# Modulation dots in the middle of each product group, their rows in the gated outputs' ring, activation sums from float32 tiles

## The chip, the core and the metric

One NeuronCore of a Trainium2 chip runs the kernel. The metric is device time in microseconds from launch to end, as the median of several runs; lower is better. Weights and inputs are float32 and lie in HBM. PE is the matmul engine, DVE the vector engine, ACT the activation engine, POOL the GpSimd engine, SP the queue that issues most loads.

## What is computed

One transformer block over 512 tokens of width 1024, batch 1. Six modulation vectors come from a small product with the conditioning vector c:

```python
mod = jnp.einsum('bd,de->be', silu(c), w_ada) + b_ada
shift1, scale1, gate1, shift2, scale2, gate2 = jnp.split(mod, 6, axis=-1)
hmix = rmsnorm(x, g_norm1) * (1 + scale1) + shift1
sb_q, sb_k, sb_v, r_q, r_k, r_v, r_g, br = jnp.split(hmix @ w_in, IN_SPLITS, axis=-1)
o_sb = stick_breaking_attention(sb_q, sb_k, sb_v)           # 16 heads of 64
o_ret = silu(r_g) * head_rmsnorm(retention(rotary(r_q), rotary(r_k) / 16, r_v))   # 4 heads, qk 256, v 512
g_sb, g_ret = jnp.split(sigmoid(br + b_branch), 2, axis=-1)
x = x + gate1 * ((g_sb * (o_sb @ w_proj_sb) + g_ret * (o_ret @ w_proj_ret)) @ w_out)
hffn = rmsnorm(x, g_norm2) * (1 + scale2) + shift2
a, u = jnp.split(hffn @ w_ffn_in, 2, axis=-1)
out = rmsnorm(x + gate2 * ((silu(a) * u) @ w_ffn_out), g_final)
```

## The kernel before

Every matmul operand is held as a high and a low part (`hi`, `lo`, both in the reduced float32 type fp32r). A product is three matmuls: hi by hi, hi by lo, lo by hi. `weight()` loads 512 KB into the ring "raw", ACT rounds it to "whi" (L206), DVE subtracts for "wlo" (L208). `high()` and `low()` (L849, L853) do the same for pieces that are sums.

A ring is a tag of a tile pool with a fixed number of buffers: "araw" has 2, "raw" 3, "whi" and "wlo" 4 each, "s" 8, "o" 8, "t" 7, "q" 8. A tile takes a buffer when one is free, and whatever fills it waits for the last reader of the tile that had it. Outside blocks under `manual_schedule` a planner orders each engine's instructions ahead of time, by program order as the priority, by free buffers, and by its own estimates of durations; at run time each engine follows that order. `tc.issue_after(ins)` puts an edge from `ins` to those instructions in its block that run on the engine of `ins`: the dots, being DVE work, come behind `ins` on DVE, but the loads of their rows do not.

The stages that matter here, in order:

- The opening (L440 to L557, order by hand): squares of x, the row scale r1, the modulation dots 0 to 7, and per 128 rows of the width the modulated activations: `h_t` (L424) writes x times gain times r1 into a "t" tile, `h_hi` and `h_lo` add the shift and split the result into `hs[n]`. For n = 0 the shift is added into the float32 tile itself.
- `sv_acts` (L860): the four sums of activation quarters S1 to S4 that the seven-product groups need. Each is built on DVE from high and low parts of `hs`, 256 columns at a time (`each`, L868 to L872), and is split by `parts` (L874).
- Four groups. Each covers `ret_gate` of one retention head (gate product L760, transposes L764, the gated outputs `ys` in four "s" tiles), `ret_proj` (its projection, summed into `spill` in DRAM), and `seven` (L973): a product of 1024 by 1024 made of seven half-size products, A11, A12, S2, S3, A22, S1, S4 in this order, with weight sums `w1` to `w7`. `b11` and `b22` are raw quarters in "s", `b12` in "araw", `b21` in "raw". Head h + 1's `ret_scores` and `ret_out` run within `seven`. The last group makes the values of the stick-breaking attention.
- The attention stage: `sb_qk` projects two heads, `heads` works through 16 heads, `mix` computes the branch gates, whose tiles are in "araw".
- The loop over `w_proj_sb` (L1120), then w_out, the second norm, the feed-forward part.

A modulation dot (`ada`, L246): a 512 KB row block of w_ada lands in a tile, DVE multiplies it by the broadcast `cact` and sums along the row (L256), reads the sum, adds the bias (L259). A pair is two such dots. Pairs 0 to 7 are in the opening; `later` holds pairs 8 to 23, which `ada_after(ins)` takes one at a time. Before the change these go: two in each `ret_gate` of heads 1 to 3, four in each `ret_proj` of heads 1 and 2, and the last two in the loop over `w_proj_sb`. All of them load into "araw".

Of the kernel before, what the change touches and what calls it, by code (L numbers as in the profile page):

```python
# [11 lines left out]
F32 = mybir.dt.float32  # L12
# [3 lines left out]
ALU = mybir.AluOpType  # L16
# [3 lines left out]
P = 128  # L20
D = 1024
S = 512
KT = D // P
# [92 lines left out]
def kernel(  # L116
# [9 lines left out]
    nc = tc.nc  # L126
# [9 lines left out]
    def nm(s):  # L136
        uid[0] += 1
        return f"{s}_{uid[0]}"
# [13 lines left out]
    def tmp():  # L152
        return apool.tile([P, S], F32, tag="t", bufs=BUFS["t"], name=nm("t"))
# [4 lines left out]
    def small(n, dt=F32):  # L158
        return cpool.tile([P, n], dt, tag=f"sm{n}{dt}", bufs=BUFS["sm"], name=nm("sm"))

    def f(ap):
        return ap.bitcast(F32)
# [15 lines left out]
    for j in range(KT):  # L178
# [9 lines left out]
    nc.vector.memset(ones, 1.0)  # L188
    eps = cpool.tile([P, 1], F32, name="eps")
    nc.vector.memset(eps, EPS)  # L190
    nc.gpsimd.affine_select(ident, ones, pattern=[[1, P]], compare_op=ALU.is_equal, fill=0.0, base=0,
                            channel_multiplier=-1)
    mod = cpool.tile([P, 48], F32, name="mod")
# [5 lines left out]
    def load_raw(src, n, tag="raw"):  # L199
        raw = wpool.tile([P, WCOLS], F32, tag=tag, bufs=BUFS[tag], name=nm(tag))  # L200
        nc.sync.dma_start(raw[:, :n], src[:, :n])
        return raw
# [32 lines left out]
    def gemm(o, w, acts, start=True, stop=True, t0=0, t1=S, ks=None):  # L235

        hi, lo = w
        n = len(acts)
        for k in ks or range(n):
            a = acts[k]  # L240
            ah, al = a if isinstance(a, tuple) else (a[:, 0, :], a[:, 1, :])
            mm3(o, hi[:, k, :], lo[:, k, :], ah[:, t0:t1], al[:, t0:t1],
                start and k == 0, stop and k == n - 1)


    def ada(n):  # L246

        pair_cols = []
        for half, c in enumerate(ADA[n]):
            if n < KT:  # L250
                raw = apool.tile([P, D], F32, tag="s", bufs=BUFS["s"], name=nm("sraw"))
                nc.sync.dma_start(raw, wada[2 * n + half])
            else:
                raw = load_raw(wada[2 * n + half], D, "araw")
            col = small(1)
            nc.vector.scalar_tensor_tensor(  # L256
                raw, raw, 1.0, cact, op0=ALU.mult, op1=ALU.mult, accum_out=col
            )
            nc.vector.tensor_add(mod[:, c : c + 1], col, sm[:, SM_BADA + c : SM_BADA + c + 1])  # L259
            pair_cols.append(mod[:, c : c + 1])  # L260
        return pair_cols
# [138 lines left out]
        cols_[n, 0] = o[:, 0:1]  # L400

    def mod_shift(n):
        sh = small(1)
        b = SM_BADA + n
        nc.scalar.activation(sh, cols_[n, 0], AF.Identity, bias=sm[:, b : b + 1])  # L405
        mods[n, 0] = sh
# [15 lines left out]
    ALL = slice(0, S)  # L422

    def h_t(n, hv=ALL):  # L424
        if n not in ts:
            ts[n] = tmp()
        nc.vector.scalar_tensor_tensor(ts[n][:, hv], xts[n][:, hv], mods[n, 1], r1[:, hv],
                                       op0=ALU.mult, op1=ALU.mult)

# [151 lines left out]
    def sb_qk(p):  # L581
        qp, kp = ps(), ps()
        gemm(qp, weight(("sq", p)), hs)
        gemm(kp, weight(("sk", p)), hs)
        sb_qk_store(p, qp, kp)

    def causal(t, c):

# [169 lines left out]
    def ret_gate(h, banks, y, sgs, between=lambda: None):  # L758
        for b, (o, sg) in enumerate(zip(banks, sgs)):
            nc.vector.scalar_tensor_tensor(sg, o, y[:, b : b + 1], sg, op0=ALU.mult, op1=ALU.mult)  # L760
        ys = []
        for e, o in enumerate((psz(), psz(), psz(), psa())):
            for b, sg in enumerate(sgs):
                nc.tensor.transpose(o[:, b * P : (b + 1) * P], sg[:, e * P : (e + 1) * P], ident)  # L764
            hl = pair("s")
            ins = split(hl[:, 0, :], hl[:, 1, :], o)
            ys.append(hl)
            between()
            if e % 2 and h:
                ada_after(ins)  # L770
        return ys

    spill = dpool.tile([8, P, S], F32, name="spill")
# [3 lines left out]
    def ret_proj(h, ys, before=lambda i: None):  # L777

        for i in range(4):
            before(i)  # L780
            hi, lo = weight(("pr", h, i))
            low = last_low[0]
            for c in range(2):
                o = ps()
                gemm(o, (hi[:, :, c * P : (c + 1) * P], lo[:, :, c * P : (c + 1) * P]), ys)
                t = otile()
                nc.scalar.activation(t, o, AF.Copy)
                if h == 0:
                    nc.sync.dma_start(spill[2 * i + c], t)
                else:  # L790
                    nc.gpsimd.dma_start(spill[2 * i + c], t, accum_op=ALU.add)
            if h in (1, 2):
                ada_after(low)


    def gate(i):

# [17 lines left out]
    gains2 = []  # L815
    later = list(range(8, 24))

    def ada_after(ins):
        with tc.issue_after(ins.ins):
            n = later.pop(0)  # L820
            sh, sc = ada(n)
            if 12 <= n < 20:
                j = n - 12
                gains2.append((gain(sc, sm[:, SM_G2 + j : SM_G2 + j + 1]), sh))
# [7 lines left out]
    def raw_quarter(tag):  # L832
        return apool.tile([P, 2 * S], F32, tag=tag, bufs=BUFS[tag], name=nm(tag))
# [16 lines left out]
        return hi  # L850

    def low(t, hi, lo):
        nc.vector.tensor_sub(lo, t, f(hi))  # L853
        return hi, lo


# [3 lines left out]
    def sv_acts():  # L860
        def part_of(lo, kh, th):
            return [hs[4 * kh + k][:, lo, th * 256 : th * 256 + 256] for k in range(4)]

        acts = {}
        for key, kh, th in (("A11", 0, 0), ("A12", 1, 0), ("A22", 1, 1)):
            acts[key] = part_of(0, kh, th), part_of(1, kh, th)

        def each(dst, op, src, kh, th, lo, swap=False):  # L868
            for k, a in enumerate(part_of(lo, kh, th)):
                d = slice(k * 256, k * 256 + 256)  # L870
                x, y = src[:, d] if src is not None else f(part_of(0, kh, th)[k]), f(a)
                nc.vector.tensor_tensor(dst[:, d], *((y, x) if swap else (x, y)), op=op)  # L872

        def parts(t, tag):  # L874
            n = 2 if tag == "o" else 4
            his, los = [], []
            for k in range(0, 4, n):
                hi, lo = (
                    apool.tile([P, n * 256], F32R, tag=tag, bufs=BUFS[tag], name=nm(tag)) for _ in range(2)
                )  # L880
                src = t[:, k * 256 : (k + n) * 256]
                nc.scalar.activation(hi, src, AF.Copy)
                nc.vector.tensor_sub(lo, src, f(hi))
                his += [hi[:, i * 256 : i * 256 + 256] for i in range(n)]
                los += [lo[:, i * 256 : i * 256 + 256] for i in range(n)]
            return his, los

        yield acts
        a21, t = raw_quarter("s"), raw_quarter("s")
        each(a21, ALU.add, None, 0, 1, 1)  # L890
        yield
        each(t, ALU.add, a21, 1, 1, 0)
        yield
        each(t, ALU.add, t, 1, 1, 1)
        acts["S1"] = parts(t, "q")
        yield
        each(t, ALU.subtract, t, 0, 0, 0)
        each(t, ALU.subtract, t, 0, 0, 1)
        yield
        acts["S2"] = parts(t, "q")  # L900
        yield
        each(a21, ALU.subtract, a21, 0, 0, 0, True)
        each(a21, ALU.add, a21, 0, 0, 1)
        yield
        acts["S3"] = parts(a21, "qp")
        each(t, ALU.subtract, t, 1, 0, 0, True)
        each(t, ALU.add, t, 1, 0, 1)
        yield
        acts["S4"] = parts(t, "o")
        yield  # L910
# [9 lines left out]
    def sv_parts(raw, dma=False, tags=("whi", "wlo")):  # L920
        hi, lo = wtile(tags[0]), wtile(tags[1])
        return split_dma(raw, hi, lo) if dma else low(raw, high(raw, hi), lo)
# [47 lines left out]
        for x, y, o in zip(a, b, out):  # L970
            nc.vector.tensor_sub(o, x, y)

    def seven(name, h, gate, store, scores=lambda: None, outs=lambda: None, first=False):  # L973

        w1, b11, b12, b22 = [], [], [], []

# [28 lines left out]
        if not first:  # L1005
            x = opening()
        w2 = [sv_parts(r) for r in b21]
        w6 = [sv_parts(t) for t in b22]
        sub(b21, b22, b21)
        store(0, 0, sv_product("A12", w2, x))  # L1010
        w7 = [sv_parts(t) for t in b12]
        for t, o in zip(p1, sv_product("S2", w6)):
            nc.vector.tensor_add(t, t, o)
        w4 = [sv_parts(t) for t in b21]
# [28 lines left out]
    sacts = next(steps)  # L1043
    for _ in steps:
        pass
    outs = ret_out(0, st, vt)
    for h in range(3):
        ys = []
# [10 lines left out]
        table_load.append(sigmoid_tables())  # L1059
        return ys  # L1060

    seven("sv", 3, last_gate, sv_store, first=True)
    act_table = table_load[0]

    diag = table(consts[:, NCON + 2 * S :])
# [14 lines left out]
            fn(d)  # L1080

    for p in PI:
        sb_qk(p)
        with tc.issue_after(act_table.ins):
            mix(1)
    fronts = {}
# [721 lines left out]
```

## Time and profile before

| | |
|---|---|
| median of 3 runs | 1115.8 us (1114.58 to 1118.3) |
| the profiled execution, its own time | 1117.28 us |
| its span, first to last instruction | 1115.6 us |
| PE busy | 1100.7 us, 99% of the span |
| DVE busy | 876.6 us, 79% |
| ACT busy | 561.5 us, 50% |
| mean DMA rate | 163 GB/s |

Rows of the profile give a line of the kernel, the engine, the operation, the tile written and the tiles read, the shape, a count, busy time and mean duration, and the idle time ahead on that engine with what ended it. A row of the waits reads: engine and line, what it waited for, total us, times, longest.

### The profile page before, as it was taken

How to read it: one execution, taken by the hardware profiler on the slowest of the kernel's cores; microseconds unless marked ns; L12 is line 12 of the kernel's file. 1: busy time of each engine (PE TensorE's matmuls, PEld its weight loads, DVE VectorE, ACT ScalarE, POOL GpSimd, SP SyncE). 2: the span in 40 equal slices, each digit the busy share in tenths (PEclk: the TensorE clock that was granted, in tenths of full speed). 3: DMA queues.
4: the chain of work that ended last, by engine and by line, in shares of the span. 5: the costliest groups of instructions: out<-in, count | busy, mean ns of one | idle time of the engine just before them, and what ended most of it. 6: DMA issues, size and time to landing. Idle time of an engine off the chain costs nothing.

```text
span 1115.6 us, 15072 instructions
## 1 busy us (share of the span) xinstructions
PE 1100.7 (99%) x5607; PEld 936.9 (84%) x5607; DVE 876.6 (79%) x1315; ACT 561.5 (50%) x926; POOL 42.2 (4%) x69
## 2 busy tenths in 40 slices
PE   8999999999999999999999999999999999999996
PEld 7888888887888888888888888889988888888886
DVE  7899756958977959377777775667999988888866
ACT  5445345444444645265465653357745544554443
POOL 0000000010020020000000000000000000000000
PEclk9999999999999999999999999999999999999999
DMA  9814431766675486876576459662444544444112
GB/s 359 303 58 151 144 121 57 241 137 207 230 179 182 165 156 212 245 213 184 163 202 173 138 181 306 214 181 58 125 140 115 150 132 132 131 115 132 57 38 77
DMA packets 60555, 181.42 MB, mean 163 GB/s; under 512 B 7489, under 2 KB 9537, under 8 KB 60481
## 3 DMA queue, kind: packets, MB, share of 16 engines
q1 hardware_dynamic: 54464, 166.30, 45.9%
q0 software_dynamic: 5472, 13.63, 7.7%
q8 instruction: 44, 0.72, 0.3%
q10 hardware_dynamic: 544, 0.52, 0.1%
q14 instruction: 31, 0.25, 0.1%
HBM read 148.97 MB, written 16.78 MB: 149 GB/s over the span
## 4 chain that ended last, share of the span: by engine, by line
PE 87%; DVE 8%; DMA 2%; ACT 2%; issue 1%; DVEq 0%; ACTq 0%
PE ps L228 64%; PE z L228 13%; PE av L228 8%; DMA araw<-wada 2%; PE ps L636 1%; DVE s L872 1%; DVE wlo L853 1%; DVE araw L256 1%; DVE wlo L208 0%; PE z L764 0%; DVE t L760 0%; DVE s L209 0%; ACT whi L849 0%; PE av L636 0%; ACT q L1187 0%
## 5 line engine op out<-in xcount | busy, mean ns | idle before, releaser
L228 PE MATMUL ps<-h,whi 128*128 128x512 f32 (+1 forms) x1026 | 294.6, 372 | 0.0
L206 ACT ACTIVATE whi<-raw 128x1024 fp32r<-128x1024 f32 (+1 forms) x104 | 108.5, 1043 | 206.6 <-PE ps L228 156.9
L228 PEld LDWEIGHTS ps<-h,whi 128*128 128x128 f32 x1026 | 185.3, 189 | 32.2 <-ACT sm L405 0.2
L228 PE MATMUL ps<-h,wlo 128*128 128x512 f32 (+1 forms) x513 | 188.0, 370 | 0.0
L208 DVE TENSOR_TENSOR wlo<-raw,whi 128x1024 fp32r<-128x1024 f32 (+1 forms) x104 | 125.0, 1202 | 65.5 <-ACT whi L206 65.0
L228 PEld LDWEIGHTS ps<-h,wlo 128*128 128x128 f32 x513 | 96.7, 189 | 16.8
L228 PE MATMUL ps<-s,whi 128*128 128x512 f32 x320 | 99.0, 390 | 0.6 <-DVE s L208 0.6
L228 PE MATMUL ps<-q,whi 128*128 128x512 f32 (+1 forms) x368 | 98.5, 386 | 0.0
L853 DVE TENSOR_TENSOR wlo<-s,whi 128x1024 fp32r<-128x1024 f32 x46 | 56.1, 1223 | 41.7 <-ACT whi L849 41.7
L228 PEld LDWEIGHTS ps<-q,whi 128*128 128x128 f32 x368 | 68.0, 188 | 13.4 <-DVE t L1325 0.2
L849 ACT ACTIVATE whi<-s 128x1024 fp32r<-128x1024 f32 x47 | 49.6, 1058 | 46.1 <-PE ps L228 38.1
L228 PE MATMUL ps<-whi,h 128*128 128x512 f32 x222 | 71.7, 391 | 0.0
L228 PEld LDWEIGHTS ps<-s,whi 128*128 128x128 f32 x320 | 60.1, 188 | 13.3 <-DVE s L208 0.9
L228 PE MATMUL ps<-s,wlo 128*128 128x512 f32 x160 | 62.3, 390 | 0.0
L228 PE MATMUL ps<-q,wlo 128*128 128x256 f32 (+1 forms) x328 | 59.4, 293 | 0.0
L228 PEld LDWEIGHTS ps<-q,wlo 128*128 128x128 f32 x328 | 48.2, 190 | 3.3
L228 PEld LDWEIGHTS ps<-whi,h 128*128 128x128 f32 x222 | 41.7, 188 | 9.5 <-ACT t L993 0.6
L256 DVE SCALAR_TENSOR_TENSOR araw<-araw,cact 128x1024 f32<-128x1024 f32 x32 | 39.1, 1229 | 9.6 <-DMA araw<-wada 9.4
L228 PE MATMUL ps<-wlo,h 128*128 128x512 f32 x111 | 43.3, 390 | 0.0
L228 PE MATMUL ps<-whi,q 128*128 128x512 f32 x128 | 40.9, 391 | 0.0
L228 PE MATMUL z<-q,q 128*128 128x256 f32 (+3 forms) x224 | 40.0, 324 | 0.0
L626 DVE TENSOR_TENSOR_SCAN s<-s,table 128x1024 f32<-128x1024 f32 x16 | 36.6, 2290 | 2.1 <-ACT s L620 2.1
(347 smaller groups left out, 2191.8 us busy)
## 6 DMA issues: line engine op xcount, KB each, us to landing
raw<-wp SPq DMA_DIRECT2D x136, 512.0 KB, 4.0
araw<-wada SPq DMA_DIRECT2D x32, 512.0 KB, 4.2
araw<-wp SPq DMA_DIRECT2D x30, 512.0 KB, 4.4
s<-wp SPq DMA_DIRECT2D x24, 512.0 KB, 5.6
sraw<-wada SPq DMA_DIRECT2D x16, 512.0 KB, 8.9
q<-qp SPq DMA_DIRECT2D x32, 256.0 KB, 4.4
spill<-o POOLq DMA_DIRECT2D x24, 256.0 KB, 4.7
s<-wp POOLq DMA_DIRECT2D x9, 512.0 KB, 6.2
```

Source lines behind the costliest of these rows:

```text
L206: nc.scalar.activation(dst_hi, src, AF.Copy, scale=scale)
L208: return (eng or nc.vector).tensor_sub(dst_lo, src, f(dst_hi))
L228: return nc.tensor.matmul(o, lhs, rhs, start=start, stop=stop, skip_group_check=True).ins
L256: nc.vector.scalar_tensor_tensor(raw, raw, 1.0, cact, op0=ALU.mult, op1=ALU.mult, accum_out=col)
L626: nc.vector.tensor_tensor_scan(n[:, ::-1], n[:, ::-1], d[:, ::-1], 0.0, op0=ALU.mult, op1=ALU.max)
L636: nc.tensor.transpose(at[bank][:, c : c + P], t[:, a + j * P : a + (j + 1) * P], ident)
L849: nc.scalar.activation(hi, t, AF.Copy)
L853: nc.vector.tensor_sub(lo, t, f(hi))
L872: nc.vector.tensor_tensor(dst[:, d], *((y, x) if swap else (x, y)), op=op)
```

## The change

**Activation sums.** `h_t` writes in place: `ts[n]` is the x tile itself, so that x times gain times r1, without its shift (for n = 0 with it), stays in the eight "o" tiles. The shifts of n = 1 to 7 become columns of one tile `shifts`, column 0 is zero. `sv_acts` builds S1 to S4 from these float32 tiles; where shifts don't cancel, a column of `shifts` goes in as the scalar of a three-operand instruction.

**Dots.** `ada` is cut in two: `ada_raw` loads the two row blocks, `ada` does the arithmetic. Pairs are now: one behind `sv_acts`, two behind the gate of head 0, two in each of the first three `seven` groups and one in the fourth, one behind each of the first two `sb_qk`, and the remaining four in the loop over `w_proj_sb`. Those within `seven` are loaded into "s" tiles (the ring of the gated outputs `ys`) ahead of `w6`, and their dots stand behind `w7`.

```diff
+    shifts = cpool.tile([P, KT], F32, name="shifts")
+    nc.vector.memset(shifts[:, 0:1], 0.0)
...
-    def ada(n):
+    def ada_raw(n, tag):
+        raws = []
+        for half in range(2):
+            raw = (apool if tag == "s" else wpool).tile([P, D], F32, tag=tag, bufs=BUFS[tag], name=nm(tag))
+            nc.sync.dma_start(raw, wada[2 * n + half])
+            raws.append(raw)
+        return raws
+
+    def ada(n, raws):
...
-        sh = small(1)
+        sh = shifts[:, n : n + 1] if n else small(1)
...
     def h_t(n, hv=ALL):
-        if n not in ts:
-            ts[n] = tmp()
+        ts[n] = xts[n]
...
     def sb_qk(p):
         qp, kp = ps(), ps()
         gemm(qp, weight(("sq", p)), hs)
         gemm(kp, weight(("sk", p)), hs)
+        low = last_low[0]
         sb_qk_store(p, qp, kp)
+        return low
...
             ys.append(hl)
             between()
-            if e % 2 and h:
-                ada_after(ins)
+        for _ in range(2 if h == 0 else 0):
+            ada_after(ins)
         return ys
...
-            if h in (1, 2):
-                ada_after(low)
...
-    def ada_after(ins):
+    def ada_early(tag="araw"):
+        n = later.pop(0)
+        return n, ada_raw(n, tag)
+
+    def ada_after(ins, loaded=None):
         with tc.issue_after(ins.ins):
-            n = later.pop(0)
-            sh, sc = ada(n)
+            n, raws = loaded or ada_early()
+            sh, sc = ada(n, raws)
...
     def low(t, hi, lo):
-        nc.vector.tensor_sub(lo, t, f(hi))
+        last_low[0] = nc.vector.tensor_sub(lo, t, f(hi))
         return hi, lo
...
-        def each(dst, op, src, kh, th, lo, swap=False):
-            for k, a in enumerate(part_of(lo, kh, th)):
-                d = slice(k * 256, k * 256 + 256)
-                x, y = src[:, d] if src is not None else f(part_of(0, kh, th)[k]), f(a)
-                nc.vector.tensor_tensor(dst[:, d], *((y, x) if swap else (x, y)), op=op)
+        def part_h(kh, th):
+            return [(xts[4 * kh + k][:, th * 256 : th * 256 + 256], shift(4 * kh + k)) for k in range(4)]
...
+        def s_sum(dst, x, sc, y, op0, op1):
+            for k in range(4):
+                d = slice(k * 256, k * 256 + 256)
+                u, v = (t[:, d] if hasattr(t, "shape") else t[k][0] for t in (x, y))
+                nc.vector.scalar_tensor_tensor(dst[:, d], u, sc[k], v, op0=op0, op1=op1)
...
+        t, s3 = raw_quarter("s"), raw_quarter("s")
+        both = cpool.tile([P, 4], F32, name="both")
+        nc.vector.tensor_add(both, shifts[:, 0:4], shifts[:, 4:8])
+        s_sum(t, a21, [both[:, k : k + 1] for k in range(4)], a22, ALU.add, ALU.add)
         yield
         acts["S1"] = parts(t, "q")
+        s_sum(t, t, low_k, a11, ALU.subtract, ALU.subtract)
         yield
         acts["S2"] = parts(t, "q")
         yield
+        for k in range(4):
+            nc.vector.tensor_sub(s3[:, k * 256 : k * 256 + 256], a11[k][0], a21[k][0])
         yield
+        acts["S3"] = parts(s3, "qp")
+        s_sum(t, a12, high_k, t, ALU.add, ALU.subtract)
         yield
         acts["S4"] = parts(t, "o")
...
         w2 = [sv_parts(r) for r in b21]
+        loaded = [ada_early("s") for _ in range(early)]
         w6 = [sv_parts(t) for t in b22]
         sub(b21, b22, b21)
         store(0, 0, sv_product("A12", w2, x))
         w7 = [sv_parts(t) for t in b12]
+        for two in loaded:
+            ada_after(last_low[0], two)
...
+    for _ in range(1):
+        ada_after(last_low[0])
     outs = ret_out(0, st, vt)
...
-    seven("sv", 3, last_gate, sv_store, first=True)
+    seven("sv", 3, last_gate, sv_store, first=True, early=1)
...
     for p in PI:
-        sb_qk(p)
+        low_ = sb_qk(p)
+        for _ in range(1):
+            ada_after(low_)
```

More of the change, by code (lines that the diff above doesn't have):

```diff
@@ L243, in gemm @@
                 start and k == 0, stop and k == n - 1)
-    def ada(n):
-        pair_cols = []
[L249 to L254, printed above, removed]
+    def ada_raw(n, tag):
[6 more added lines that the diff above has]
+    def ada(n, raws):
+        pair_cols = []
+        for raw, c in zip(raws, ADA[n]):
             col = small(1)
@@ L781, in ret_proj @@
             hi, lo = weight(("pr", h, i))
-            low = last_low[0]
             for c in range(2):
@@ L866, in sv_acts, with shift @@
             acts[key] = part_of(0, kh, th), part_of(1, kh, th)
-        def each(dst, op, src, kh, th, lo, swap=False):
-            for k, a in enumerate(part_of(lo, kh, th)):
-                d = slice(k * 256, k * 256 + 256)
-                x, y = src[:, d] if src is not None else f(part_of(0, kh, th)[k]), f(a)
-                nc.vector.tensor_tensor(dst[:, d], *((y, x) if swap else (x, y)), op=op)
+        def part_h(kh, th):
+            return [(xts[4 * kh + k][:, th * 256 : th * 256 + 256], shift(4 * kh + k)) for k in range(4)]
+        def shift(n):
+            return shifts[:, n : n + 1]
         def parts(t, tag):
@@ L886, in parts @@
             return his, los
+        def s_sum(dst, x, sc, y, op0, op1):
[3 more added lines that the diff above has]
+                nc.vector.scalar_tensor_tensor(dst[:, d], u, sc[k], v, op0=op0, op1=op1)
+        a11, a12, a21, a22 = part_h(0, 0), part_h(1, 0), part_h(0, 1), part_h(1, 1)
+        low_k = [shift(k) for k in range(4)]
+        high_k = [shift(4 + k) for k in range(4)]
         yield acts
-        a21, t = raw_quarter("s"), raw_quarter("s")
-        each(a21, ALU.add, None, 0, 1, 1)
+        t, s3 = raw_quarter("s"), raw_quarter("s")
+        both = cpool.tile([P, 4], F32, name="both")
+        nc.vector.tensor_add(both, shifts[:, 0:4], shifts[:, 4:8])
+        s_sum(t, a21, [both[:, k : k + 1] for k in range(4)], a22, ALU.add, ALU.add)
         yield
-        each(t, ALU.add, a21, 1, 1, 0)
-        yield
-        each(t, ALU.add, t, 1, 1, 1)
         acts["S1"] = parts(t, "q")
-        yield
-        each(t, ALU.subtract, t, 0, 0, 0)
-        each(t, ALU.subtract, t, 0, 0, 1)
+        s_sum(t, t, low_k, a11, ALU.subtract, ALU.subtract)
         yield
@@ L901, in sv_acts @@
         yield
-        each(a21, ALU.subtract, a21, 0, 0, 0, True)
-        each(a21, ALU.add, a21, 0, 0, 1)
+        for k in range(4):
+            nc.vector.tensor_sub(s3[:, k * 256 : k * 256 + 256], a11[k][0], a21[k][0])
         yield
-        acts["S3"] = parts(a21, "qp")
-        each(t, ALU.subtract, t, 1, 0, 0, True)
-        each(t, ALU.add, t, 1, 0, 1)
+        acts["S3"] = parts(s3, "qp")
+        s_sum(t, a12, high_k, t, ALU.add, ALU.subtract)
         yield
@@ L971, in sub, with seven @@
             nc.vector.tensor_sub(o, x, y)
-    def seven(name, h, gate, store, scores=lambda: None, outs=lambda: None, first=False):
+    def seven(name, h, gate, store, scores=lambda: None, outs=lambda: None, first=False, early=2):
         w1, b11, b12, b22 = [], [], [], []
```

## Prediction

> **What bounds the kernel now.** I read the page's busy times first, then who the matmul engine waited for, then the stretches that the change touches, then the chain of waits.
>
> ```profile
> span 1115.6 us, 15072 instructions
> PE 1100.7 (99%) x5607; PEld 936.9 (84%) x5607; DVE 876.6 (79%) x1315; ACT 561.5 (50%) x926; POOL 42.2 (4%) x69
> ```
>
> PE is idle for 1115.6 - 1100.7 = 14.9 us of the span. No edit here removes or adds a matmul, so the change can only win part of those 14.9 us, or add to them. The waits of PE say which part has a producer that the change touches:
>
> ```profile
> PE z L228 <- DVE mod L452: 3.6, 1, 3.6
> PE ps L228 <- DVE wlo L853: 0.9, 1, 0.9
> PE ps L228 <- DVE s L208: 0.6, 1, 0.6
> PE z L764 <- DVE t L760: 0.3, 1, 0.3
> PE z L228 <- ACT s L206: 0.3, 1, 0.3
> ```
>
> The 3.6 us are the start of the program, which the edits leave alone. Three waits end with DVE: a low half of a weight piece (L853), a low half of a gated output (L208), the gate's product (L760). The table by stage places them (columns: stretch, length, busy us of PE, PEld, DVE, ACT, POOL, clock, DMA share, GB/s):
>
> ```profile
> 75.00:101.00 26.00, 25.67 (x120) 21.15 (x119) 25.55 (x63) 14.15 (x23) 0.84 (x2) 1.00 0.38 138
> 101.00:161.00 60.00, 60.00 (x269) 49.56 (x268) 41.08 (x47) 25.34 (x34) 0.00 (x0) 1.00 0.39 127
> 194.00:255.00 61.00, 61.00 (x278) 50.60 (x277) 47.51 (x62) 26.54 (x35) 6.96 (x8) 1.00 0.69 188
> 255.00:289.00 34.00, 33.14 (x153) 27.32 (x152) 29.81 (x62) 16.20 (x27) 2.48 (x4) 1.00 0.52 176
> 385.00:435.00 50.00, 49.43 (x220) 40.60 (x218) 36.27 (x50) 24.32 (x35) 6.92 (x9) 1.00 0.76 194
> 435.00:475.00 40.00, 39.85 (x179) 32.92 (x178) 19.64 (x28) 15.82 (x25) 0.38 (x9) 1.00 0.78 230
> 690.00:712.00 22.00, 22.00 (x99) 18.23 (x98) 18.27 (x28) 8.37 (x10) 0.00 (x0) 1.00 0.90 307
> 712.00:758.00 46.00, 46.00 (x268) 40.83 (x267) 28.55 (x42) 19.79 (x26) 2.60 (x3) 1.00 0.50 138
> ```
>
> PE loses 0.33 us in 75 to 101, 0.86 in 255 to 289, 0.57 in 385 to 435 and 0.15 in 435 to 475: 1.91 us in all. Where PE loses nothing DVE has room (18.9 us of 60 in 101 to 161); in 75 to 101 it is busy for 25.55 of 26 us. The chain of waits in 247 to 270 shows how the largest loss arises:
>
> ```profile
> 247.85 3.44 DMA araw<-wada
> 251.38 1.24 DVE araw L256 x2
> 252.64 4.36 DMA araw<-wada
> 257.02 1.25 DVE araw L256 x2
> 258.28 6.13 DMA araw<-wada
> 264.43 1.24 DVE araw L256 x2
> 267.69 1.14 DVE wlo L853
> 268.87 1.21 PE ps L228 x4
> ```
>
> This is the ring "araw" of two buffers: a load lands, a modulation dot reads it, and only then may the next load go. DVE works in order, so the low half at 267.69 stands behind a dot that waited for its load, and PE stands behind that low half. Load, dot, load, dot is the releaser from 247.85 to 265.67.
>
> A stall costs somewhat more than its idle time, as two rows of the timeline there show:
>
> ```profile
> 267.51 0.50 PE L228 MATMUL ps<-whi,q 128*128 128x512 f32 x1
> 268.87 0.51 PE L228 MATMUL ps<-wlo,q 128*128 128x512 f32 x1 [0.86 <-DVE wlo L853]
> ```
>
> ```profile
> 101.58 59.97 PE ps L228 x264
> ```
>
> Undisturbed, a matmul starts every 59.97 / 264 = 0.227 us. Here 1.36 us lie between two starts: 1.13 lost for 0.86 of idle, 0.27 us more.
>
> **The change part by part. Activation sums.** The rows of the vector work concerned, mean ns of one behind the comma:
>
> ```profile
> L872 DVE TENSOR_TENSOR s<-s,h 128x256 f32<-128x256 f32 x24 | 8.3, 420 | 0.0
> L872 DVE TENSOR_TENSOR s<-h,s 128x256 f32<-128x256 f32 x8 | 2.9, 420 | 0.0
> L872 DVE TENSOR_TENSOR s<-h 128x256 f32<-128x256 f32 x4 | 1.7, 474 | 0.0
> L1682 DVE SCALAR_TENSOR_TENSOR o<-o,gfh,t 128x256 f32<-128x256 f32 x8 | 3.4, 479 | 0.0
> L256 DVE SCALAR_TENSOR_TENSOR araw<-araw,cact 128x1024 f32<-128x1024 f32 x32 | 39.1, 1229 | 9.6 <-DMA araw<-wada 9.4
> L256 DVE DVE_READ_ACCUMULATOR araw<-araw,cact 128x1 f32 x32 | 2.7, 83 | 0.0
> L259 DVE TENSOR_TENSOR mod<-sm,sm 128x1 f32<-128x1 f32 x32 | 4.9, 154 | 0.0
> L853 DVE TENSOR_TENSOR wlo<-s,whi 128x1024 fp32r<-128x1024 f32 x46 | 56.1, 1223 | 41.7 <-ACT whi L849 41.7
> ```
>
> Removed: 36 additions, 8.3 + 2.9 + 1.7 = 12.9 us of DVE. Added: 12 operations with a column as scalar, for which L1682 is the nearest row (3.4 / 8 = 0.425 us each, 5.1 us), 4 plain subtractions at 2.9 / 8 = 0.36 (1.5 us), and the addition of two columns (0.15 us). DVE saves 12.9 - 6.7 = 6.2 us, between 5.1 (0.479 us for each of the 16) and 7.0 (0.36 for each). [...] I take 6.2.
>
> The gain written in place (h_t) is the same instruction on another address; its memset is one column. The float tiles now live until the sums: they hold their eight "o" buffers longer, but the next user of "o" is the fourth sum's own parts, as before. Zero; what could show otherwise is an ACT copy waiting for an "o" buffer.
>
> **Dots.** One dot costs 1.229 + 0.083 + 0.154 = 1.47 us of DVE. All 32 remain, 46.9 us, so only their places and loads count.
>
> - Ahead of the first group come one pair after the sums and two after the first gate. The first adds 2.9 us where 6.2 fall away: DVE is 3.3 us earlier at the gate's products, and the 0.33 us in 75 to 101 go. The others add 5.9 us from about 104 on, where 18.9 are idle. They hold back b12's two loads, which share "araw". The same pattern, two pairs behind a gate and ahead of b12, stands in 194 to 255, where PE lost 0.00 of 61 us. Zero; if that cover failed, one load's 6.13 us.
> - In each group the pairs of gate and projection go (four pairs in the second half of groups 1 and 2); two pairs come behind w7, with four loads into "s" as soon as the projection's last matmul frees the gated outputs. These loads pass the second b22 load on SP, which isn't used before the last product. The load-dot chain above disappears: the four loads are under way at once, and two products (2 x 24 matmuls x 0.227 = 10.9 us) lie between their start and the dots' turn. DVE's load after w7 falls by four dots in 255 to 289, 5.9 us, and the 0.86 us go; in group 2 the same four dots go ahead of the last gate, for whose low halves (L208) PE waited, so the 0.57 us go. What is late next is ACT's copy of the S1 product (the 0.15 us at 435); I leave that in. New waits: the three "s" tiles of the next scores stand behind the four dots. Their turn is again two products, 10.9 us, after w7, and four dots are 5.9. Zero; bound again 6.13.
> - Two pairs move behind the first attention projections: 5.9 us into a stretch where DVE is busy for 19.64 of 40. Zero.
> - The loop over w_proj_sb carries four pairs rather than two. This is the dear place:
>
> ```profile
> 688.74 1.22 DVE L256 SCALAR_TENSOR_TENSOR araw<-araw,cact 128x1024 f32<-128x1024 f32 x1 [2.05 <-DMA araw<-wada]
> 691.28 1.22 DVE L208 TENSOR_TENSOR wlo<-raw,whi 128x1024 fp32r<-128x1024 f32 x1
> 693.53 0.39 PE L228 MATMUL ps<-q,wlo 128*128 128x512 f32 x1
> 698.44 1.22 DVE L208 TENSOR_TENSOR wlo<-raw,whi 128x1024 fp32r<-128x1024 f32 x1
> 704.41 0.39 PE L228 MATMUL ps<-q,wlo 128*128 128x512 f32 x1
> ```
>
> Between the old pairs a weight's low half is done at 692.50 and used at 693.53, a lead of 1.0 us; two weights later the lead is 704.41 - 699.66 = 4.75. The new pairs fall behind that point: 5.9 us of dots, against 3.7 us of idle DVE in 690 to 712 and 17.4 in 712 to 758. The lead shrinks and holds. Zero; bound, two more waits of 2.05, 4.1 us.
>
> **Sum.** 0.33 + 0.86 + 0.57 = 1.76 us of idle, and 3 x 0.27 = 0.81 of restarts: 2.6 us less. The profiled execution took 1117.28 us for its span of 1115.6, and comes to 1114.7. It lies 1.5 us above the median of 1115.8, so the median comes to 1113.2, 0.23% less. A measurement of this kernel tells about 0.3%, 3.3 us, from no change; I call that the same.
>
> **The rivals.** *All the small stalls go.* If the 0.15 us and the 0.3 of L206 also vanish with their restarts, the gain is 2.57 + 0.45 + 0.54 = 3.6 us: 1112.2, just faster. For it: both are waits for ACT copies, and ACT in turn waits for DVE work that the dots delay or reorder. Against: no dot stands near L206's. The forecast itself is within 0.7 us of the bound, so the scatter of a measurement can carry it there too. [...] Chance 0.29.
>
> *The projection loop becomes DMA- and DVE-bound.* Four more loads of 512 KB are 2.1 MB. At 307 GB/s with the DMA 0.90 busy they put 6.8 us ahead of the weights in SP's queue, and the dots put 5.9 us ahead of the low halves, 12.7 together. The lead of 4.75 us and the 3.7 of idle DVE cover 8.4; PE would wait 4.3. If the idle DVE time cannot be used, 8.0. With the 2.6 won that is 1117.5 to 1121.2, slower in the upper part. For it: the lead of 1.0 between the old pairs, and dots waiting for loads there. Against: weights are loaded three deep. It decides once a weight's low half ends after 704. Chance 0.24 for slower, with everything else that could stall PE by over 5.9 us.
>
> *The dots don't leave the second half.* The order on each engine is planned from program order and buffers; if the "s" loads land late, the new pairs sit where the old ones did and the stalls stay: 1115.8. Chance 0.09, the same.
>
> **Numbers.** The forecast has 0.38, the third rival 0.09: same 0.47, faster 0.29, slower 0.24. The forecast's own range is 1112.5 to 1115.8 (the bound of 0.3%; nothing won). The whole range is 1110.9 to 1119.6: down to 1.3 us below the first rival for scatter, up to the middle of the second.
>
> **What would show it.** L872 gone, sixteen 256-wide operations of 0.36 to 0.48 us in its place; DVE below 25 us in 75 to 101. PE's waits for L853, L208 and L760 gone. Dots read "s" tiles with no idle ahead of them. In the projection loop four pairs of dots and no wait of PE for a low half; such a wait would prove the slower rival, and PE's old waits in the list the third.

## The result: slower by a quarter per cent

| | before | after |
|---|---|---|
| median | 1116.7 us (10 runs) | 1119.3 us (10 runs) |
| lowest to highest | 1114.6 to 1118.3 | 1117.9 to 1120.5 |
| profiled execution, its own time | 1117.28 us | 1119.87 us |
| span | 1115.6 us | 1118.2 us |

After over before is 1.0025, with an interval of 1.0015 to 1.0034. Forecast was 0.23% less, called no change, with 1112.5 to 1115.8 us as its own range; the rival of the projection loop had put 1117.5 to 1121.2.

The page of after:

```profile
span 1118.2 us, 15055 instructions
PE 1102.5 (99%) x5607; PEld 937.8 (84%) x5607; DVE 872.0 (78%) x1297; ACT 560.8 (50%) x926; POOL 40.4 (4%) x69
```

PE has the same 5607 matmuls and is busy for 1.8 us longer, so part of the loss isn't idle time: matmuls took longer. PE's waits (total us, times, longest) begin with the 3.5 us of the start (3.6 before), and go on:

```profile
PE ps L230 <- ACT h L208: 1.3, 1, 1.3
PE ps L230 <- DVE h L210: 0.8, 1, 0.8
```

The three waits that the prediction wanted to remove (a low half of a weight piece, one of a gated output, the gate's product) are gone. Two new ones have come, both for "h", the split of a merged tile of the projection loop (`ms`). The table by stage of after has the same columns as before:

```profile
75.00:101.00 26.00, 25.89 (x122) 21.32 (x121) 22.39 (x49) 14.68 (x24) 1.00 (x2) 1.00 0.49 176
255.00:289.00 34.00, 34.00 (x165) 28.68 (x164) 25.34 (x47) 17.71 (x29) 1.62 (x4) 1.00 0.24 78
385.00:435.00 50.00, 49.99 (x221) 41.02 (x219) 35.19 (x46) 25.02 (x36) 7.37 (x18) 1.00 0.68 177
435.00:475.00 40.00, 40.00 (x180) 33.27 (x179) 22.91 (x38) 15.44 (x28) 0.00 (x0) 1.00 0.82 240
690.00:712.00 22.00, 22.00 (x99) 18.22 (x98) 19.07 (x35) 5.72 (x7) 0.00 (x0) 1.00 0.91 303
712.00:758.00 46.00, 43.86 (x241) 37.98 (x239) 29.38 (x36) 21.39 (x26) 2.60 (x3) 0.96 0.60 174
```

In the first four stretches PE now loses 0.12 us, where it lost 1.91. All that and more is given back in 712 to 758: 2.14 us of idle, and a granted clock of 0.96. Counted along the matmuls, the 3201st starts at 686.95 before and at 684.88 after, 2.1 us earlier; the 3401st at 732.29 and 734.54, 2.25 later. So these 200 matmuls take 45.33 us before and 49.67 after: 4.3 us are lost here. The timeline of PE there:

```profile
722.73 0.39 PE L230 MATMUL ps<-h,wlo 128*128 128x512 f32 x1
724.41 0.49 PE L230 MATMUL ps<-h,whi 128*128 128x512 f32 x1 [1.29 <-ACT h L208]
725.75 0.79 PE L230 MATMUL ps<-h,whi 128*128 128x512 f32 x1 [0.85 <-DVE h L210]
726.33 0.63 PE L230 MATMUL ps<-h,wlo 128*128 128x512 f32 x1
```

The product is the first of w_out: it reaches the last merged tile and has neither its high nor its low part. From the second wait on a matmul takes 0.63 us, not 0.39:

```profile
726.00:729.30 3.30, 3.30 (x9) 2.60 (x10) 2.30 (x3) 2.57 (x3) 0.00 (x0) 0.51 0.50 164
```

Nine matmuls in 3.30 us at a clock of 0.51, where 14.5 go at 0.227 us. The trace has the half clock from 725.79 on for 3.41 us. From the matmul at 725.75 to the one at 729.28 it is eight starts in 3.53 us, where 8 x 0.227 = 1.82 would do: 1.7 us. The 4.3 us are 2.14 of idle, 1.7 of half clock, and a remainder of 0.5, which two restarts at the 0.27 us of the prediction would fill by estimate.

Why "h" is late shows the chain of waits of after, around the two waits:

```profile
708.75 0.42 SPq L203
...
709.23 6.63 DMA raw<-wp
...
715.96 1.07 ACT whi L208
717.05 1.24 DVE wlo L210
718.30 4.37 DMA raw<-wp
722.78 1.07 ACT whi L208
723.87 1.22 DVE wlo L210
725.09 0.61 DVE h L210
```

Read it backwards. The low part of the last merged tile (725.09) stands on DVE behind the low half of a w_out weight (723.87), its high part on ACT behind that weight's rounding (722.78). The weight had only just landed. Its load could start when an earlier w_out weight had left the "raw" ring (718.30), and that one was issued at 709.23, right behind the first w_out weight at 708.75. The timeline of SP's queue says why so late, first after:

```profile
696.76 0.53 SPq L203 DMA_DIRECT2D raw<-wp  x1
697.89 1.99 SPq L252 DMA_DIRECT2D araw<-wada  x2
...
704.62 1.67 SPq L1233 DMA_DIRECT2D araw<-wp  x2
708.37 0.33 SPq L1143 DMA_DIRECT2D t<-gspill  x1
708.75 1.37 SPq L203 DMA_DIRECT2D raw<-wp  x3
```

and before:

```profile
693.50 0.42 SPq L201 DMA_DIRECT2D raw<-wp  x1
...
697.19 0.43 SPq L1215 DMA_DIRECT2D araw<-wp  x1
...
698.92 0.43 SPq L1215 DMA_DIRECT2D araw<-wp  x1
699.40 0.43 SPq L201 DMA_DIRECT2D raw<-wp  x1
...
703.13 0.90 SPq L201 DMA_DIRECT2D raw<-wp  x2
```

The two loads "araw<-wp" (L1233 after, L1215 before) belong to the feed-forward stage, which comes after w_out. They share the ring "araw" with the dots, and they stand in SP's queue ahead of three w_out weights, though those have another ring. With two pairs in the loop "araw" was free by 697.19; with four it is free when the last dots are done, at 705.93. Between these loads and the weights stands one more load, of gspill (L1143), the branch gates for the loop. It waits for a "t" tile until DVE, behind the last dots, has added up a tile of the loop (L1145). So from 696.76 to 708.75 no weight is issued, and the last of the waits is that of the gspill load. What waits is named in the waits of SP's queue, 690 to 712:

```profile
SPq L1143 <- DVE t L1145: 4.0, 3, 2.0
...
SPq L1233 <- DVE mod L264: 1.2, 1, 1.2
SPq L1233 <- DVE araw L261: 0.9, 1, 0.9
```

### The profile page after: what moved, and what is told of

The parts are those of the page before. It is cut to its first block, busy times and chain, and to the rows that moved or that the text cites. A ratio compares the mean times of both kernels' runs of the same rounds, so it can differ in the third digit from the quotient of the medians.

```text
span 1118.2 us, 15055 instructions
## 1 busy us (share of the span) xinstructions
PE 1102.5 (99%) x5607; PEld 937.8 (84%) x5607; DVE 872.0 (78%) x1297; ACT 560.8 (50%) x926; POOL 40.4 (4%) x69
## 4 chain that ended last, share of the span: by engine, by line
PE 90%; DVE 4%; DMA 3%; ACT 2%; issue 1%; SPq 0%; DVEq 0%; ACTq 0%
PE ps L230 65%; PE z L230 14%; PE av L230 8%; DMA araw<-wada 1%; PE ps L642 1%; DMA raw<-wp 1%; DVE araw L261 0%; PE z L770 0%; DMA gspill<-g 0%; DVE wlo L210 0%; PE av L642 0%; DMA t<-spill 0%; ACT q L1205 0%; DVE o L1700 0%; DVE h L1515 0%
## 5 line engine op out<-in xcount | busy, mean ns | idle before, releaser
L208 ACT ACTIVATE whi<-raw 128x1024 fp32r<-128x1024 f32 (+1 forms) x104 | 108.8, 1046 | 184.6 <-PE ps L230 133.8
L230 PEld LDWEIGHTS ps<-s,whi 128*128 128x128 f32 x320 | 60.1, 188 | 12.7 <-DVE s L210 0.3
L230 PEld LDWEIGHTS z<-q,q 128*128 128x128 f32 x224 | 34.8, 189 | 3.0 <-DVE q L210 0.2
```

The lines of the kernel that those rows point to most:

```text
L208: nc.scalar.activation(dst_hi, src, AF.Copy, scale=scale)
L230: return nc.tensor.matmul(o, lhs, rhs, start=start, stop=stop, skip_group_check=True).ins
```

## The experiments

Three theories: the two extra pairs in the projection loop cost the time through the place of their loads in SP's queue (the queue theory, mine); they cost it by their 5.9 us of DVE and 2.1 MB of loads as such, whatever the queue; or the loss comes from the new sums or from the pairs in the groups. Each ratio below is to the kernel before, timed beside the version; its medians in the three sets of runs were 1116.0, 1116.9 and 1116.2 us. The traces give a finer measure of the place: the 200 matmuls from the 3201st to the 3401st take 45.33 us where PE doesn't wait among them.

**The two halves of the change.** The kernel before with the new sums alone (`shifts`, `h_t` in place, `s_sum` in `sv_acts`):

> Sums from float tiles alone; all dots where they were before. Theory A: only the small stall at 99.8 us shrinks, 0.2 to 0.6 us less than before, about 1116.3, and no wait in the projection loop. Theory B with the sums as the cause: a new wait, 1118 or more.

1117.1 us, ratio 1.0005 (0.9996 to 1.0013). The small wait near 100 is gone, the others stay: PE waits 0.86 us for a low half at 269.11 and 0.78 us at 386.69. The dots alone, with the old sums (`ada_raw`, `ada_early`, `early` in `seven`, and the new places of `ada_after`):

> Dots moved as in the change; sums as before. Theory A: the stalls at 269 and 386 us gone, the stall and half clock near 724 there, a little slower than the changed kernel since the sums' 6 us of vector work stay ahead of group 0: 1119 to 1120. Theory B with the sums as the cause: below 1116.

1119.6 us, ratio 1.0028 (1.0019 to 1.0037): the whole loss. Its PE timeline has the same two waits, though no half clock came behind them here; the 200 matmuls take 47.41 us:

```profile
723.60 0.50 PE L228 MATMUL ps<-h,whi 128*128 128x512 f32 x1 [0.62 <-ACT h L206]
724.94 0.50 PE L228 MATMUL ps<-h,whi 128*128 128x512 f32 x1 [0.84 <-DVE h L208]
```

**Two pairs out of the loop, into the attention stage.**

```diff
     for p in PI:
         low_ = sb_qk(p)
         for _ in range(1):
             ada_after(low_)
...
-            sb_qk(p)
+            low_ = sb_qk(p)
+            if p in (2, 3):
+                ada_after(low_)
```

> The changed kernel, with pairs 20 and 21 of the dots moved from the projection loop to behind the third and fourth attention projections, so that the loop carries two pairs as it did before. Theory A (the two extra pairs in the loop cause the whole loss, all else in the change wins): PE's wait near 724 us, 2.1 us, and the half clock behind it are gone; about 2.2 us less than before, 1114.5. Theory B (the loss comes from elsewhere, the loop only shows it): the wait stays and the time is about 1119. Theory C (any two pairs cost the same wherever they stand): the wait moves into the attention stage, about 1119.

1117.3 us, ratio 1.0012 (1.0003 to 1.0021). The waits at 724 are gone (45.33 us for the 200 matmuls), and others come:

```profile
PE av L230 <- DVE s L210: 1.4, 2, 0.9
```

They lie at 487 and 513: a head's weights of attention are low halves on DVE too. That the two pairs make these waits is likely but not shown: the next version, without pairs there, has such a wait of 0.64 us too, at 627. The run agrees with either theory of the loop. Of the third theory the sums fall with the two runs before; the pairs in the groups don't make the waits at 724, and a later version that keeps them all loses nothing.

**The loop's two costs apart.** All dots stay, but the rows of the last two pairs are loaded ahead of the loop, into the ring "v" of the attention's values, which is free by then:

```diff
-            raw = (apool if tag == "s" else wpool).tile([P, D], F32, tag=tag, bufs=BUFS[tag], name=nm(tag))
+            raw = (apool if tag in ("s", "v") else wpool).tile([P, D], F32, tag=tag, bufs=BUFS[tag], name=nm(tag))
...
     ms = []
+    early_v = [ada_early("v") for _ in range(2)]
     for d in range(8):
...
         if later:
             ada_after(ins)
+        elif early_v:
+            ada_after(ins, early_v.pop(0))
```

> The changed kernel, with the rows of the last two pairs loaded into the value ring v, which is free once the last attention head is out, rather than into araw; their dots stay in the projection loop. If the loss is one of queue order (the loads wait in SP's queue for dots to free araw, and the weights of the next product wait behind them): the wait near 724 goes or falls below 0.5 us, 1115 to 1116. If it is the dots' 5.9 us on the vector engine, or the 2.1 MB of extra transfers as such: it stays, about 1119.

1116.0 us, ratio 1.0003 (0.9994 to 1.0011), and no loss at 724 (45.33 us). The reverse: the loads stay, and the last two pairs' dots leave out all but 16 of their 1024 columns.

```diff
+            w_ = 16 if n >= 22 else D
             nc.vector.scalar_tensor_tensor(
-                raw, raw, 1.0, cact, op0=ALU.mult, op1=ALU.mult, accum_out=col
+                raw[:, :w_], raw[:, :w_], 1.0, cact[:, :w_], op0=ALU.mult, op1=ALU.mult, accum_out=col
             )
```

> The changed kernel; the dots of the last two pairs multiply 16 columns rather than 1024 (so gate2's last four column blocks are wrong), their loads stay. The vector engine is rid of 4 x 1.1 = 4.3 us in the projection loop. If the dots' time on the vector engine makes the wait near 724 us: the wait goes, and the time is about 1116. If it is the loads in SP's queue or the transfers as such: the wait stays, 1118 to 1119.

1116.7 us, ratio 0.9997 (0.9988 to 1.0006). The three w_out weights are still issued late, from 707.46 on, and one of the two waits remains:

```profile
725.03 0.50 PE L230 MATMUL ps<-h,whi 128*128 128x512 f32 x1 [0.84 <-DVE h L210]
```

The 200 matmuls take 46.77 us, 1.44 more than undisturbed, a loss that the ratio doesn't resolve. Last, the last two pairs without loads, with full dots on the tiles of the pair before in place of their own rows:

```diff
+    kept = [None]
...
-            n, raws = loaded or ada_early()
+            if later and later[0] >= 22:
+                n, raws = later.pop(0), kept[0]
+            else:
+                n, raws = loaded or ada_early()
+            kept[0] = raws
```

> The changed kernel; the last two pairs load nothing and their dots, as long as before, read the tiles of pair 21 (so gate2's last four column blocks are wrong). SP's queue and the DMA are rid of four loads, 2.1 MB. If the loads make the wait near 724 us: it goes, about 1116. If the dots' 5.9 us on the vector engine make it: it stays, 1118 to 1119.

1116.4 us, ratio 1.0002 (0.9993 to 1.0011), no wait of PE for "h" (45.33 us). Full dots without their loads cost nothing here; loads with hardly any dots still cost 1.44 us, against 2.08 with full dots in the trace of the dots alone. So the loads are the main cause, and the dots' time adds to it. In the version without loads the planner also put the first two w_out weights (695.93 and 701.35) ahead of the feed-forward loads (703.10). Whether it is the loads' bytes or their place in the queue these three therefore don't tell.

**The kernel before, twice more.**

> The kernel before, unchanged, for a second trace of it. Its timed spans fall into two heaps, 1113.4 to 1114.7 and 1115.2 to 1116.4 us, and the trace of the prediction was of the upper heap. If the stalls at 269 and 386 us belong to the upper heap alone, a trace with a span near 1114 shows them gone or half as long, and the change had less to win than 2.6 us in a usual execution. If they are in every execution, it shows 0.9 and 0.6 us of waits as the first did, and the heaps differ elsewhere.

> The same kernel once more, for a third trace: the same two expectations.

1116.2 and 1115.8 us, spans of 1114.5 and 1114.1. The waits of the first:

```profile
PE ps L228 <- DVE s L208: 0.8, 1, 0.8
PE z L764 <- DVE t L760: 0.3, 1, 0.3
```

The second has 0.3 in place of the 0.8. The largest wait of the prediction, 0.86 us for L853 at 269, is in neither. It isn't an accident of one execution either: the trace of the new sums alone, with all dots in their old places, has it at 269.11. Two of these four traces have it, the two with the longer spans (1115.6 and 1116.5).

**Queue or bytes.** All four pairs stay in the loop, with all loads and dots. Only the two feed-forward loads are issued from POOL's queue:

```diff
-        nc.sync.dma_start(r, wp[WIDX["ff", p, half, c]])
+        (nc.gpsimd if p == 0 and tag == "araw" else nc.sync).dma_start(r, wp[WIDX["ff", p, half, c]])
```

> The changed kernel with only one difference: the two loads of the next stage that share the dots' ring (L1233, p = 0, tile araw) are issued from POOL's queue instead of SP's. All four pairs stay in the projection loop, same dots, same bytes. Theory A (SP's queue order: these loads wait for the ring, and the weights of w_out stand behind them): the weights land near 704 to 710 as before the change, the low halves of the last two merged tiles are ready in time, the waits of PE at 724 to 727 go or fall below 0.8 us in all, and the time falls by 1.5 us or more, to 1116 to 1118. Theory B (the dots' own 5.9 us of DVE and the 2.1 MB more of loads, whatever the queue): the waits remain at 1.5 to 2.5 us in all and the time stays within 0.5 us of 1119.3.

1115.7 us, ratio 0.9999 (0.9990 to 1.0008). The same DVE work, the same bytes, and SP's queue now gives out the first two w_out weights 5 us earlier than in the changed kernel, if not as early as before the change (699.40 and 703.13):

```profile
703.67 0.90 SPq L203 DMA_DIRECT2D raw<-wp  x2
709.35 0.33 SPq L1143 DMA_DIRECT2D t<-gspill  x1
709.77 0.38 SPq L203 DMA_DIRECT2D raw<-wp  x1
```

The chain of waits from 690 to 731 has nothing else in it than matmuls:

```profile
689.92 41.25 PE ps L230 x182
```

The queue theory is shown, and that of dots and bytes as such falls: nothing is left of the 1.0025 once the first weights don't stand behind loads that wait. Two points stay open. The planner, which orders SP's queue too, has put these weights ahead of the gspill load as well, so the shares of the feed-forward loads and of that load aren't told apart. And its order for ACT and DVE shifts by a few instructions in this loop, which wasn't tried apart either. At the last merged tile, though, that order is the same in both traces: ahead of the tile's split stand the rounding and the low half of the same w_out weight, at 718.63 and 720.60 here, at 722.78 and 723.87 in the changed kernel.

**The changed kernel, once more.**

> The changed kernel again, one more trace. If the wait at 724 belongs to the kernel and the half clock behind it only to some executions: 1.5 to 2.3 us of idle PE at 723 to 727 again, and either a span near 1118.3 with 3.4 us at half clock right behind it, or a span near 1116.3 without. If the wait itself is one execution's accident: no wait there and a span near 1114.3.

1119.1 us, a span of 1117.4. The waits are there again, smaller, and no half clock behind them:

```profile
725.29 0.49 PE L230 MATMUL ps<-h,whi 128*128 128x512 f32 x1 [0.35 <-ACT h L208]
726.63 0.50 PE L230 MATMUL ps<-h,whi 128*128 128x512 f32 x1 [0.85 <-DVE h L210]
```

Against the trace with the loads on POOL's queue, this one loses 1.8 us here and 1.6 in the opening, where it has 3.41 us of half clock from 16.73 on:

```profile
0.00:30.00 30.00, 25.59 (x107) 19.91 (x108) 23.02 (x44) 15.84 (x29) 0.54 (x5) 0.94 0.94 356
```

So the wait belongs to the kernel; the half clock to some executions, and not always at this place.

**A placement without the loop.** The loop has two pairs again; one more goes behind the sums, one more into the fourth group.

```diff
-    for _ in range(1):
+    for _ in range(2):
         ada_after(last_low[0])
...
-    seven("sv", 3, last_gate, sv_store, first=True, early=1)
+    seven("sv", 3, last_gate, sv_store, first=True, early=2)
```

> The changed kernel with the two extra pairs taken out of the projection loop again: one goes behind the activation sums, where the sums left 3 us, one into the fourth seven-product group, loaded into the s ring. The loop has two pairs, as before the change. If two pairs too many in the projection loop are the whole loss: no wait of PE at 724, no half clock there, 2 to 2.5 us below the changed kernel, 1114 to 1116 us and span near 1114.2. If any pair moved into the groups or behind the sums costs as much wherever it stands (no room anywhere, as the attention stage had none): a new wait of 0.5 to 1.5 us near 100 or near 385, and 1116 to 1117.

1117.1 us, ratio 1.0007 (0.9998 to 1.0016). There is no wait at 724, but a new one of the size that the second outcome names, at another place (423.83). Its chain of waits near the end of the fourth group:

```profile
416.58 2.29 DVE s L261 x4
...
420.28 2.29 DVE s L261 x4
...
422.64 1.15 DVE wlo L859
```

The low half that the next product needs stands behind two pairs at once, and PE waits 1.05 us. "Two products lie between" held for the first three groups, not here; what makes the difference isn't shown.

None of these versions beats the kernel before by more than its interval.

## Why the prediction was wrong

**Sums: right.** Their rows after:

```profile
L898 DVE SCALAR_TENSOR_TENSOR s<-o,both,o 128x256 f32<-128x256 f32 x4 | 1.8, 512 | 0.0
L898 DVE SCALAR_TENSOR_TENSOR s<-s,shifts,o 128x256 f32<-128x256 f32 x4 | 1.7, 478 | 0.0
L898 DVE SCALAR_TENSOR_TENSOR s<-o,shifts,s 128x256 f32<-128x256 f32 x4 | 1.7, 477 | 0.0
L915 DVE TENSOR_TENSOR s<-o 128x256 f32<-128x256 f32 x4 | 1.4, 413 | 0.0
```

With the column addition they come to 6.8 us; 6.7 were forecast. The three-operand form costs 477 to 512 ns beside 413 for the plain one, 64 to 99 ns more; at 1024 columns the two took 1229 and 1223 ns before the change (L256, L853). PE's idle time in 75 to 101 fell from 0.33 to 0.11.

**Groups: the mechanism right, the gain mis-sized.** The dots on "s" tiles have no idle time ahead of them, those on "araw" still have some:

```profile
L261 DVE SCALAR_TENSOR_TENSOR araw<-araw,cact 128x1024 f32<-128x1024 f32 x18 | 21.8, 1221 | 4.7 <-DMA araw<-wada 4.6
L261 DVE SCALAR_TENSOR_TENSOR s<-s,cact 128x1024 f32<-128x1024 f32 x14 | 16.6, 1220 | 0.0
```

The 1.91 us of PE's idle time became 0.12 in the four stretches. But the term of 0.86 us isn't in every execution: two more traces of before don't have it. Their waits on the change's path are 1.1 and 0.7 us, not the 1.76 that the prediction summed. In such an execution about half of the 2.6 us was to be had or less: the changed kernel's 3201st matmul starts 2.1 us ahead of the first trace of before, but 1.0 and 0.6 us ahead of the other two (685.84 and 685.46). The version with the loads on POOL's queue shows it: it has no wait in these places, and its median is 0.5 us below that of before beside it, 1116.2, within the interval.

**Projection loop: the step that failed.** The prediction put the cost at zero, because "the lead shrinks and holds", a lead of a weight's low half over the matmul that reads it. Two things were wrong in that step. First, the 1.0 us paired rows by shape. Counted in order, one low half to a product, the low half at 691.28 belongs to the next product, whose first use of it is this row of PE's timeline before:

```profile
698.97 0.39 PE L228 MATMUL ps<-q,wlo 128*128 128x512 f32 x1
```

The lead was 6.5 us (the 4.75 is paired wrongly in the same way), and no low half of the loop's own weights was late after the change (PE is busy for 22.00 of 22 us in 690 to 712). Second, it counted what the moved dots put on DVE, and in the rival their loads' bytes, but not what stood behind them in SP's queue: loads that need tiles which the dots hold up, and weights behind those. The damage came one stage on, at w_out's first product: 2.14 us of waits and 4.3 us in all in the profiled execution, 1.8 in the second trace of after. The prediction also had the change act on PE's 14.9 idle us alone; the 3.41 us of half clock made PE's busy time longer (1102.5 us beside 1100.7).

The slower rival came near the place, and its 4.3 us are what the trace lost there, by luck. It did have the weights held up in SP's queue, but by 12.7 us of bytes and dots against 8.4 of slack, and that is not what happened: with the same bytes and dots nothing is lost once two loads change queues (ratio 0.9999). The 4.3 us came out as 2.1 of wait, 1.7 of a half clock that it didn't have, and 0.5 besides.

**The sum.** The two profiled executions differ by the gain of 2.1 up to the loop, the 4.3 lost behind it, and 0.3 to 0.4 at the end: 2.6 between the spans. Over the ten runs the medians differ by 2.6 as well, which is chance: an execution as the second and third trace of before has less to gain, and one of after without the half clock loses less. **The other rivals.** *All small stalls go* had half of its premise: the 0.15 us at 435 are gone, the 0.3 us for ACT (L206 before, L208 after) remain, and there is no gain; *the dots don't leave the second half* is refuted by the waits. (The whole range ends at 1119.6 as "the middle of the second", which is 1119.4.)

## What to carry to other kernels

When work is moved, follow its loads in the issuing queue too: ask which later load needs the ring that it keeps busy, and which transfers with free buffers stand behind that one. If such a load must wait, issue it from a queue in which nothing urgent stands behind it; here the ratio to before went from 1.0025 to 0.9999 by it. And before summing small waits, look at a second execution: a stall of a few tenths to one microsecond may be in some executions and not in others, as the 0.86 us at 269 were in one of three traces of before.

## What the runs showed of the hardware

Two idle stretches of 1.29 and 0.85 us, with one matmul between them, were followed by 3.41 us at half clock (the profiled execution of after); stretches of 0.62 and 0.84 (the dots alone), and of 0.35 and 0.85 (the second trace of after), were not. In the changed kernel 5 of 10 runs had a mean clock of 0.996 or less, of the kernel before none of 35, 5 of 21 and 1 of 21 in the three sets of runs beside the experiments; but in the version without loads, whose trace has no wait here, it was 4 of 11. What decides it in an execution stays open, and that these waits bring it on isn't shown: a profiled execution had its half clock in the opening instead.
